# One class of 21 places for weights and working tiles, and the down stage's products into h issued later

## The chip, the cores and the metric

The kernel runs on one core of a Trainium2 chip. A core has five engines that run side by side, each through its own queue in order: TensorE (PE; its weight loads are shown as PEld), VectorE (DVE), ScalarE (ACT), GpSimd (POOL) and SyncE (SP). Here SyncE only issues transfers from memory to the on-chip buffer; 16 DMA engines move them. The metric is the device time of one execution in microseconds, lower is better. Three runs of the kernel before took 2260.67, 2268.3 and 2269.16 us, median 2268.3.

## The reference

256 tokens of width 1024 in float32 pass through two layers and then a third block:

```
for l in 0, 1:
    h = h + hybrid_mixer(rmsnorm(h))       # dilated + windowed attention, branches w_a, w_b, output w_o
    h = h + expert_choice_ffn(rmsnorm(h))  # 16 experts, each takes its 32 best tokens
h = rmsnorm(h)
token mixer: gated linear recurrence + long convolution (projections w2z, w2q, w2v, w2h, w2g ..., output w2o)
MoE: 32 experts in 4 groups, 2 experts per token; final norm

def expert_choice_ffn(h, w_router, w_gate, w_up, w_down):
    aff = softmax(h @ w_router); gate, idx = top_k(aff.T, 32)
    a, u = xe @ w_gate, xe @ w_up          # per expert, 1024 -> 1024 each
    ye = (silu(a) * u) @ w_down            # per expert, 1024 -> 1024
    return zeros.at[idx].add(gate * ye)
```

All expert weights are read in full: 128 MB of gate and up and 64 MB of down weights in each of the two layers, and about as much again in the MoE.

## The kernel before

**Stages.** Layer 0's mixer, layer 0's experts, layer 1's mixer, layer 1's experts, token mixer, MoE. An expert stage has two parts. In the first, for every expert, eight chunks of `w_eg` (gate and up together, 128 x 2048 floats, 1 MB, 8 KB per partition) are multiplied by the tokens the expert chose (L774). In the second, the down stage, for four column quarters q and four groups y of four experts, four chunks of `w_ed` are multiplied by the hidden values (L816), the result is scaled and split into two parts (`yd`, ScalarE L109 and VectorE L110), multiplied by the scatter matrix `Ge` (L824, the products into h), and added to h (VectorE, L827).

**Woven work.** Layer 0's down stage contains layer 1's first projections: `ahead.steps` is a generator of projection steps (weights `wk`, split by ScalarE, VectorE or GpSimd at L98 and L99, products at L118 to L120). From q = 1 on, 8, 8 and 7 steps are issued behind the products into h of groups 0, 1 and 2.

**Places.** A chunk is loaded into a place of the on-chip buffer, and the load waits until that place's last reader is done. Before, there are classes "w" (5 places) and "x" (4) and ten single places of the same 8 KB that also hold working tiles (`hTa`, `qa`, `V`, `G`, `hgw`, `hn`, `ob` ...). `chunk()` takes its class from a list written by hand (`K.spare` first, then the cycle `K.ring`). Some chunks are loaded in quarters (`quarters`, L68, 256 KB each) into places of the small classes P, PT, wh and wl. P holds attention probabilities, wh and wl hold the split weights of the projections, so a quarter there waits for the splits and products of the mixer before.

**What sets the order.** The program is written as one sequence; a list scheduler with a simulated time line places instructions on each engine's queue. SyncE then issues its loads in that order, at most eight behind each other on eight completion semaphores: a load also waits for the one eight places ahead of it to land, and a load that waits holds all behind it. Lines: `chunk` L48, `piece` with its load L60, `quarters` L68, experts L755 to L833, MoE chunks L1377 and L1422.

Of the kernel before, what the change touches and what calls it, by code (L numbers as in the profile page):

```python
# [9 lines left out]
F = mybir.dt.float32  # L10
FR = mybir.dt.float32r
# [8 lines left out]
L = 2  # L20
# [12 lines left out]
class Core:  # L33
    def __init__(self, ctx, tc, A):
# [6 lines left out]
        self.ring, self.spare, self.idle = list("wwxwx"), [], ()  # L41
# [16 lines left out]
    def piece(self, src, tag):  # L58
        t = self.sb.tile([128, PW], F, name="w", tag=tag, bufs=RING.get(tag, 1))
        self.nc.sync.dma_start(out=t[:, :src.shape[1]], in_=src)  # L60
        return t

# [12 lines left out]
    def t(self, shape, name, bufs=1, tag=None, dt=F):  # L75
        return self.sb.tile(shape, dt, name=name, tag=tag or name, bufs=bufs)
# [134 lines left out]
class Ahead:  # L211
# [6 lines left out]
    def start(self):  # L218
# [5 lines left out]
        self.raw = K.t([128, 8, T], "raw", RING["x"], tag="x")  # L224
# [65 lines left out]
RING = {"w": 5, "x": 4}  # L290
# [25 lines left out]
def mixer(K, h, l, ada, first=None, ahead=None):  # L316
# [142 lines left out]
    if ahead:  # L459
        K.ring = list("wwwwwx")  # L460

    def window():
        for pair in range(8):
            po = pos[pair % 2]
            PTs = []
            for half in range(2):
# [6 lines left out]
                sk = K.sink[:, l, hd, :]  # L473
# [45 lines left out]

    QS = [K.t([128, 8, T], "q0", tag="qc", dt=FR), K.t([128, 8, T], "q1", RING["x"], tag="x", dt=FR)]  # L520
    kx = K.t([128, 8, T], "kx", RING["x"], tag="x", dt=FR)
# [82 lines left out]
def spread_gate(K, g):  # L604
    nc = K.nc
    if g == 0:
        K.gt = K.t([128, PW], "gt", tag="x", bufs=RING["x"]).rearrange("p (a b) -> p a b", a=2)
# [10 lines left out]
def first_loads(K):  # L618
# [3 lines left out]
    K.sink, K.bgate = K.load("sink", [128, L, 16, 2]), K.load("bgate", [128, L, 16])  # L622
# [3 lines left out]
    K.iota, K.fold = K.load("iota", [128, 65]), K.load("fold", [128, 96])  # L626
# [54 lines left out]
def experts(K, h, l, mix, ada, prep, ahead=None):  # L681
# [74 lines left out]
    K.ring = list("wwxwx")  # L756
    K.spare = [None] * 7 + ["V", "qa", "qb", "qc"] + ([] if ahead else ["ob"]) + ["hgw"] + (["G"] if ahead else [])
    K.spare += [("P",) * 4] + ([] if ahead else ["hn"]) + [("wh", "wh", "wh", "wl"), ("wl", "wl", "PT", "PT")]
    hid, Ge = [], []
    gw = K.t([128, 4], "gw4")  # L760
    for e in range(NE):
        if e == 2:
            for _ in gather(1):
                pass
            K.ring = ["w", "x", "w", "V", "w", "x", "qb", "w", "qc", "x", "w", "hgw", "x", "G"] if ahead else list("wwxwx") + ["qc"]
        oh, xT = ohs[e // 8], xTs[e // 8]
        gu = K.bank("mm")
        for k in range(KD):
# [3 lines left out]
            w = K.chunk(A["w_eg"][l, e, k])  # L772
# [34 lines left out]
    K.ring = ["w", "x", "w", "qc", "w", "x", "w", "x", "w"] if ahead else ["w", "x", "w", "qc", "w", "hTa", "x", "w", "qa", "w"]  # L807
    for q in range(4):
        for y in range(NE // 4):
            ws = [K.chunk(A["w_ed"][l, q, 4 * y + x]) for x in range(4)]  # L810
            dn = K.bank("acc")
            for fb in range(8):
                for x in range(4):
# [7 lines left out]
            p = K.bank("sc")  # L821
            for tt in range(2):
                for i in range(2):
                    nc.tensor.matmul(p[:, tt * T:(tt + 1) * T], lhsT=Ge[y // 2][:, y % 2, tt * 128:(tt + 1) * 128],  # L824
                                     rhs=yd[:, i], start=(i == 0), stop=(i == 1))
            hs = h[:, :, q * T:(q + 1) * T]
            nc.vector.tensor_add(hs, p.rearrange("p (t c) -> p t c", t=2), hs)  # L827
# [5 lines left out]
    K.ring = list("wwxwx")  # L833
# [22 lines left out]
def context(K):  # L856
# [24 lines left out]
    s0 = K.t([128, PW], "S0", tag="x", bufs=RING["x"])  # L881
# [814 lines left out]
```

## Time and profile before

| | |
|---|---|
| median of three runs | 2268.3 us |
| profiled execution | 2264.96 us |
| its span (first to last instruction) | 2263.2 us |
| mean granted TensorE clock | 0.906 of 2.4 GHz |
| TensorE busy | 1810.0 us (80%) |
| VectorE, ScalarE, GpSimd busy | 786.9, 588.7, 220.7 us |
| moved from memory | 745.77 MB, mean 330 GB/s |
| median from issue to landing, w_eg and w2eg chunks | 15.6 and 19.8 us |

The stages lie in the span thus: layer 0's mixer to about 277 us, its expert products from 290 to 625, its woven down stage from 625 to 816; layer 1's mixer to 977, its experts to about 1480; the token mixer to about 1780; the MoE to the end at 2263.2. Because the limits differ from stage to stage, the shares of the whole span say little; the rows below are taken stage by stage. GB/s tells how far the transfers are the limit in a stretch, busy time how far an engine is, and the timelines tell when SyncE issued what.

### The profile page before, as it was taken

What the parts mean: (1) busy time and instruction counts of PE and PEld (TensorE: products, weight loads), DVE (VectorE), ACT (ScalarE), POOL (GpSimd) and SP (SyncE); (2) the same over time, 40 slices, a digit from 0 to 9 for tenths busy, and PEclk for the clock granted to TensorE, in tenths of its full rate; (3) what the DMA queues carried; (4) which work ended last, traced back from release to release, by engine and by line L of the source; (5) the groups of instructions that cost most, each with busy time, mean ns of one, the idle gap of its engine ahead of it and who ended that gap; (6) DMA issues with size and microseconds to landing.
All of it is one profiled execution on the core that took longest, in us unless ns stands there. A gap on an engine that the chain in (4) does not pass through costs nothing.

```text
span 2263.2 us, 30298 instructions
## 1 busy us (share of the span) xinstructions
PE 1810.0 (80%) x12172; PEld 1026.7 (45%) x12172; DVE 786.9 (35%) x1823; ACT 588.7 (26%) x1182; POOL 220.7 (10%) x179
## 2 busy tenths in 40 slices
PE   8999997666699998996778566669999877776765
PEld 8877741111277765842234223248888522121211
DVE  5766620000145589631211111147647511111112
ACT  5545510000033345620124200036325310000000
POOL 2111200000011122200000000024224100000000
PEclk9999997777799999998899777889999999999999
DMA  7446599999999944679999999982336799999996
GB/s 301 136 165 238 216 377 421 421 421 422 422 375 409 386 163 187 233 278 366 411 416 415 371 420 421 420 336 105 119 115 233 300 411 421 421 421 421 422 421 277
DMA packets 113626, 748.87 MB, mean 331 GB/s; under 512 B 14695, under 2 KB 15112, under 8 KB 25416
## 3 DMA queue, kind: packets, MB, share of 16 engines
q1 hardware_dynamic: 112936, 745.82, 81.7%
q8 instruction: 98, 1.61, 0.3%
q10 hardware_dynamic: 544, 1.05, 0.1%
q14 instruction: 48, 0.39, 0.1%
HBM read 745.77 MB, written 1.05 MB: 330 GB/s over the span
## 4 chain that ended last, share of the span: by engine, by line
PE 44%; DMA 27%; issue 21%; DVE 5%; ACT 2%; POOL 0%; POOLq 0%; SPq 0%; DVEq 0%; ACTq 0%
DMA w<-in_w_eg 15%; DMA w<-in_w_ed 7%; PE mm L118 7%; PE mm L120 7%; PE mm L119 6%; PE mm L774 4%; PE acc L816 4%; DMA w<-in_w2z 1%; DVE wl L99 1%; PE acc L493 1%; PE acc L901 1%; PE sc L841 1%; DMA w<-in_ada 1%; PE acc L1181 1%; PE sc L478 1%
## 5 line engine op out<-in xcount | busy, mean ns | idle before, releaser
L774 PE MATMUL mm<-w,xT 128*32 128x512 f32 x2048 | 325.0, 743 | 131.4 <-DMA w<-in_w_eg 131.3
L98 ACT ACTIVATE wh<-w 128x512 fp32r<-128x512 f32 x384 | 239.5, 630 | 314.5 <-PE mm L119 237.1
L118 PE MATMUL mm<-hTa,wh 128*128 128x256 f32 x960 | 282.5, 296 | 8.3 <-DVE qa L242 2.4
L120 PE MATMUL mm<-hTa,wl 128*128 128x256 f32 x960 | 276.4, 291 | 4.5 <-DVE wl L99 4.2
L119 PE MATMUL mm<-hTb,wh 128*128 128x256 f32 x960 | 274.4, 287 | 1.2 <-DVE hTb L1004 1.2
L99 DVE TENSOR_TENSOR wl<-w,wh 128x512 fp32r<-128x512 f32 x286 | 220.1, 775 | 100.4 <-ACT wh L98 97.5
L1429 PE MATMUL mm<-w,xT 128*32 128x512 f32 x1024 | 174.1, 618 | 61.5 <-DMA w<-in_w2eg 60.9
L99 POOL TENSOR_TENSOR wl<-w,wh 128x512 fp32r<-128x512 f32 x98 | 129.7, 1324 | 917.2 <-ACT wh L98 411.8
L774 PEld LDWEIGHTS mm<-w,xT 128*32 128x32 f32 x2048 | 59.1, 123 | 352.3 <-DMA w<-in_w_eg 245.3
L816 PE MATMUL acc<-w,hid 128*32 128x256 f32 x2048 | 167.0, 436 | 59.9 <-DMA w<-in_w_ed 59.9
L118 PEld LDWEIGHTS mm<-hTa,wh 128*128 128x128 f32 x960 | 182.8, 191 | 28.4 <-issue 13.5
L120 PEld LDWEIGHTS mm<-hTa,wl 128*128 128x128 f32 x960 | 182.5, 191 | 14.3 <-issue 6.2
L119 PEld LDWEIGHTS mm<-hTb,wh 128*128 128x128 f32 x960 | 183.5, 191 | 5.4 <-issue 2.4
L816 PEld LDWEIGHTS acc<-w,hid 128*32 128x32 f32 x2048 | 76.8, 124 | 136.2 <-DMA w<-in_w_ed 68.2
L1470 PE MATMUL acc<-w,work 128*32 128x512 f32 x512 | 103.4, 681 | 36.4 <-DMA w<-in_w2ed 35.0
L1429 PEld LDWEIGHTS mm<-w,xT 128*32 128x32 f32 x1024 | 33.6, 110 | 172.1 <-DMA w<-in_w2eg 126.1
L175 POOL TENSOR_TENSOR rs<-rs,mhalf 128x2 f32<-128x2 f32 x9 | 6.7, 748 | 1010.7 <-DVE rs L174 1010.5
L790 DVE TENSOR_TENSOR hid<-tp,sg 128x256 f32<-128x256 f32 x32 | 13.6, 424 | 221.0 <-ACT sg L789 221.0
L88 DVE COPY gs<-mm 128x512 f32<-128x512 f32 x16 | 11.1, 692 | 199.6 <-PE mm L774 199.6
L110 DVE SCALAR_TENSOR_TENSOR yd<-acc,gw,yd 128x256 fp32r<-128x256 f32 x32 | 15.5, 483 | 179.4 <-ACT yd L109 179.4
L789 ACT ACTIVATE sg<-tp 128x256 f32<-128x256 f32 x32 | 12.3, 383 | 227.5 <-PE tp L786 227.4
L109 ACT ACTIVATE yd<-acc,gw 128x256 fp32r<-128x256 f32 x32 | 15.1, 473 | 213.2 <-PE acc L816 213.2
(469 smaller groups left out, 2504.4 us busy)
## 6 DMA issues: line engine op xcount, KB each, us to landing
w<-in_w_eg SPq DMA_DIRECT2D x250, 1024.0 KB, 15.6
w<-in_w_ed SPq DMA_DIRECT2D x128, 1024.0 KB, 14.1
w<-in_w2eg SPq DMA_DIRECT2D x126, 1024.0 KB, 19.8
w<-in_w2ed SPq DMA_DIRECT2D x63, 1024.0 KB, 19.8
w<-in_ada SPq DMA_DIRECT2D x24, 1024.0 KB, 6.3
w<-in_w_in SPq DMA_DIRECT2D x22, 1024.0 KB, 7.1
w<-in_wk SPq DMA_DIRECT2D x20, 1024.0 KB, 9.3
w<-in_w_b SPq DMA_DIRECT2D x8, 1024.0 KB, 6.2
```

Of the source, the lines that this page charges most:

```text
L98: self.hi = nc.scalar.activation(hi, src, AF.Copy)
L99: (nc.gpsimd if n in self.idle or n % 4 == 3 else nc.vector).tensor_tensor(lo, src, hi.bitcast(F), OP.subtract)
L118: mm(out, lhsT=l[0], rhs=r[0], start=start, stop=False)
L119: mm(out, lhsT=l[0], rhs=r[1], start=False, stop=False)
L120: mm(out, lhsT=l[1], rhs=r[0], start=False, stop=stop)
L478: nc.tensor.matmul(p[:, sl], lhsT=q[hq], rhs=KL[hq, kv // 2, :], start=False, stop=True)
L493: nc.tensor.matmul(po[half * 64:half * 64 + 64, :T], lhsT=V[:, kt, c:c + 64], rhs=PTs[half][:, kt * 256:(kt + 1) * 256], start=(kt == 0), ...
L774: nc.tensor.matmul(gu[32 * j:32 * j + 32, :], lhsT=xT[:, k, (e % 8) * CAP:(e % 8 + 1) * CAP], rhs=w[:, j * 512:(j + 1) * 512], start=(k == ...
L816: nc.tensor.matmul(dn[32 * x:32 * x + 32, :T], lhsT=hid[e // 8][:, e % 8, f, hh * 32:hh * 32 + 32], rhs=ws[x][:, fb * T:(fb + 1) * T], sta ...
L841: nc.tensor.matmul(p[:, :T], lhsT=hn[:, tt, kb * 128:(kb + 1) * 128], rhs=oh[:, tt].rearrange("p a b -> p (a b)"), start=(tt == 0), stop=( ...
L1429: nc.tensor.matmul(gu[o:o + 32, :], lhsT=xT[:, k, y:y + CAP2], rhs=ws[x][:, (2 * kk + j) * 512:(2 * kk + j + 1) * 512], start=(k == 0), st ...
L1470: nc.tensor.matmul(dn[32 * x:32 * x + 32, :], lhsT=hid[x][:, c, :], rhs=wd[x][:, c * 512:(c + 1) * 512], start=(c == 0), stop=(c == 3), ti ...
```

## The change

The classes "w" and "x" and the ten single places become one class "W" with 21 places. A tile whose old name is in `WHOLE`, and every whole chunk, takes the next place of that class in turn; the lists `K.ring` are gone. `K.spare` is now the same at every expert stage and the MoE: eight whole chunks, two in quarters ("P","P","wh","wh") and ("wh","wl","wl","wl"), and then whole ones. The first 21 chunks of an expert stage (19 whole, two in quarters), and the first 19 of the MoE (17 whole), are requested in one go ahead of the stage's products. In the down stage the products into h and the add are a function `add`: in layer 0 from q = 1 on it is called behind 6, 6, 6 and 5 woven steps, elsewhere behind the next group's expert products. Room comes from smaller scratch tiles. The core of the diff:

```diff
 def chunk(self, src):
-        tag = self.spare.pop(0) if self.spare else None
-        if tag is None:
-            tag = self.ring[self.nchunk % len(self.ring)]
-            self.nchunk += 1
-        if isinstance(tag, tuple):
-            return self.quarters(src, tag)
-        return self.piece(src, tag)
...
+        if self.spare and (tags := self.spare.pop(0)):
+            return self.quarters(src, tags)
+        t = self.sb.tile([128, PW], F, name="w", tag="W", bufs=PLACES)
         self.nc.sync.dma_start(out=t[:, :src.shape[1]], in_=src)
         return t
...
-RING = {"w": 5, "x": 4}
+WHOLE = {"x", "hTa", "hTb", "qa", "qb", "qc", "V", "G", "hgw", "hn", "ob"}
+PLACES = 21
+SPARE = [None] * 8 + [("P", "P", "wh", "wh"), ("wh", "wl", "wl", "wl")]
...
-    K.ring = list("wwxwx")
-    K.spare = [None] * 7 + ["V", "qa", "qb", "qc"] + ([] if ahead else ["ob"]) + ["hgw"] + (["G"] if ahead else [])
-    K.spare += [("P",) * 4] + ([] if ahead else ["hn"]) + [("wh", "wh", "wh", "wl"), ("wl", "wl", "PT", "PT")]
+    K.spare = SPARE[:]
+
+    ws = [K.chunk(A["w_eg"][l, i // KD, i % KD]) for i in range(PLACES)]
...
-            w = K.chunk(A["w_eg"][l, e, k])
+            w = ws.pop(0) if ws else K.chunk(A["w_eg"][l, e, k])
...
+    def add(q, y, yd):
+        p = K.bank("sc")
+        for tt in range(2):
+            for i in range(2):
+                nc.tensor.matmul(p[:, tt * T:(tt + 1) * T], lhsT=Ge[y // 2][:, y % 2, tt * 128:(tt + 1) * 128],
+                                 rhs=yd[:, i], start=(i == 0), stop=(i == 1))
+        hs = h[:, :, q * T:(q + 1) * T]
+        nc.vector.tensor_add(hs, p.rearrange("p (t c) -> p t c", t=2), hs)
...
+            if late:
+                add(*late)
             yd = K.t([128, 2, T], "yd", NP, tag="PT", dt=FR)
             K.split_to(yd[:, 0], yd[:, 1], dn[:, :T], gw[:, y:y + 1])
...
-            if ahead and q and y < 3:
-                for _ in islice(ahead.steps, (8, 8, 7)[y]):
+            late = (q, y, yd)
+            if ahead and q:
+                for _ in islice(ahead.steps, (6, 6, 6, 5)[y]):
                     pass
+                add(*late)
+                late = None
...
+    K.spare = SPARE[:]
+    K.pre = [K.chunk(A["w2eg"][0 + 2 * i + x, c]) for i in range(2) for c in range(4) for x in range(2)]
+    K.pre += [K.chunk(A["w2ed"][x, 0]) for x in range(3)]
```

SyncE's queue at the end of layer 0's mixer, before (L60 is a whole chunk, L68 a quarter; `xN` is N such rows):

```order
56 L60 DMA w<-in_w_eg 128x2048 x2
57 L60 DMA w<-in_ada 128x2048
58 L60 DMA w<-in_w_eg 128x2048 x7
59 L68 DMA w_3379<-in_w_eg 128x512
60 L68 DMA w_3385<-in_w_eg 128x512
61 L68 DMA w_3391<-in_w_eg 128x512
62 L68 DMA w_3381<-in_w_eg 128x512
63 L68 DMA w_3393<-in_w_eg 128x512
64 L68 DMA w_3383<-in_w_eg 128x512
65 L60 DMA w<-in_w_eg 128x2048 x15
```

And after (L53 whole, L64 quarter):

```order
46 L64 DMA w_3246<-in_w_eg 128x512
47 L64 DMA w_3248<-in_w_eg 128x512
48 L53 DMA w<-in_w_o 128x2048 x2
49 L53 DMA w<-in_ada 128x2048 x3
50 L64 DMA w_3256<-in_w_eg 128x512
51 L64 DMA w_3250<-in_w_eg 128x512
52 L64 DMA w_3258<-in_w_eg 128x512
53 L64 DMA w_3252<-in_w_eg 128x512
54 L64 DMA w_3260<-in_w_eg 128x512
55 L64 DMA w_3254<-in_w_eg 128x512
56 L53 DMA w<-in_w_eg 128x2048 x126
```

All eight quarters of w_eg now stand ahead of its first whole chunk; two of them, in places of class P, also ahead of the last two w_o chunks. At the end of layer 1's mixer the rows are the same.

SyncE's queue at the end of the token mixer, before; seven whole w2eg chunks stand above these rows in ones and twos between the loads of the token mixer's own weights:

```order
209 L60 DMA w<-in_w2eg 128x2048 x3
210 L60 DMA w<-in_ada 128x2048 x3
211 L68 DMA w_13743<-in_w2eg 128x512
212 L68 DMA w_13737<-in_w2eg 128x512
213 L60 DMA w<-in_w2eg 128x2048
214 L68 DMA w_13745<-in_w2eg 128x512
215 L68 DMA w_13739<-in_w2eg 128x512
216 L68 DMA w_13747<-in_w2eg 128x512
217 L599 DMA gb<-in_gtb 128x512
218 L68 DMA w_13741<-in_w2eg 128x512
219 L68 DMA w_13749<-in_w2eg 128x512
220 L68 DMA w_13751<-in_w2eg 128x512
```

And after, where no w2eg stands above these rows:

```order
155 L53 DMA w<-in_ada 128x2048 x4
156 L64 DMA w_13596<-in_w2eg 128x512
157 L64 DMA w_13590<-in_w2eg 128x512
158 L64 DMA w_13598<-in_w2eg 128x512
159 L64 DMA w_13592<-in_w2eg 128x512
160 L64 DMA w_13600<-in_w2eg 128x512
161 L599 DMA gb<-in_gtb 128x512
162 L64 DMA w_13586<-in_w2eg 128x512
163 L64 DMA w_13594<-in_w2eg 128x512
164 L64 DMA w_13588<-in_w2eg 128x512
165 L53 DMA w<-in_w2eg 128x2048 x14
166 L53 DMA w<-in_w2ed 128x2048 x3
```

TensorE's queue in layer 0's down stage, the first group of q = 1, before (L816 the experts' down products, L824 the products into h, L118 to L120 the woven projections, `sc` and `acc` banks of the accumulator):

```order
1749 L119 MATMUL mm<-hTb,wh 128x256
1750 L120 MATMUL mm<-hTa,wl 128x256
1751 L816 MATMUL acc<-w,hid 32x256 x35
1752 L824 MATMUL sc<-yd,Ge_3821 128x256 x4
1753 L118 MATMUL mm<-hTa,wh 128x256
1754 L119 MATMUL mm<-hTb,wh 128x256
```

And after, the third group of q = 1 (L824 is now the down products, L810 the products into h, L117 to L119 the projections):

```order
1683 L119 MATMUL mm<-hTa,wl 128x256
1684 L824 MATMUL acc<-w,hid 32x256 x32
1685 L117 MATMUL mm<-hTa,wh 128x256
1686 L118 MATMUL mm<-hTb,wh 128x256
...
1706 L118 MATMUL mm<-hTb,wh 128x256
1707 L119 MATMUL mm<-hTa,wl 128x256
1708 L810 MATMUL sc<-yd,Ge_4308 128x256 x4
1709 L117 MATMUL mm<-hTa,wh 128x256
```

The products into h moved from directly behind their group's down products to behind some twenty rows of projections.

## Rows read from the trace of the kernel before

**Rows 1.** The page: bytes moved in 40 slices (GB/s), and one row of the DMA issues.

```profile
GB/s 301 136 165 238 216 377 421 421 421 422 422 375 409 386 163 187 233 278 366 411 416 415 371 420 421 420 336 105 119 115 233 300 411 421 421 421 421 422 421 277
...
w<-in_w_eg SPq DMA_DIRECT2D x250, 1024.0 KB, 15.6
```

**Rows 2.** Stage windows: length, busy us of each engine, PEclk, DMA share, GB/s.

```profile
270.00:300.00 30.00, 25.68 (x142) 11.73 (x142) 15.20 (x51) 7.15 (x14) 0.71 (x1) 0.83 0.68 255
300.00:400.00 100.00, 80.03 (x487) 24.46 (x488) 9.40 (x24) 8.60 (x17) 0.00 (x0) 0.80 1.01 418
500.00:625.00 125.00, 76.80 (x548) 21.43 (x541) 9.68 (x17) 6.89 (x14) 0.00 (x0) 0.76 1.01 421
625.00:816.00 191.00, 180.55 (x1660) 141.41 (x1659) 103.76 (x166) 62.60 (x110) 28.07 (x22) 0.98 0.91 369
966.00:977.00 11.00, 10.53 (x48) 6.89 (x47) 3.50 (x6) 3.31 (x7) 1.29 (x1) 1.00 0.48 172
977.00:1040.00 63.00, 55.46 (x334) 24.45 (x332) 17.29 (x49) 11.50 (x23) 0.71 (x1) 0.92 0.81 313
1040.00:1240.00 200.00, 147.76 (x832) 58.95 (x832) 35.04 (x83) 49.66 (x75) 0.69 (x1) 0.87 1.01 415
1240.00:1440.00 200.00, 126.52 (x1076) 54.30 (x1072) 22.73 (x50) 24.64 (x38) 0.00 (x0) 0.79 0.98 407
1780.00:1820.00 40.00, 33.92 (x224) 14.52 (x222) 13.81 (x59) 10.50 (x19) 0.71 (x1) 0.91 0.82 313
2000.00:2200.00 200.00, 143.56 (x788) 42.16 (x782) 32.47 (x62) 14.61 (x27) 0.00 (x0) 0.97 1.01 421
```

**Rows 3.** SyncE's timeline, layer 0: start us, us, then the operation.

```profile
113.08 0.33 SPq L60 DMA_DIRECT2D w<-in_w_eg  x1
...
199.94 0.33 SPq L60 DMA_DIRECT2D w<-in_w_eg  x1
...
230.73 35.59 SPq L60 DMA_DIRECT2D w<-in_w_eg  x7
266.90 3.37 SPq L68 DMA_DIRECT2D w<-in_w_eg  x6
278.76 34.48 SPq L60 DMA_DIRECT2D w<-in_w_eg  x15
```

**Rows 4.** SyncE's timeline before the experts of layer 1.

```profile
851.49 0.33 SPq L60 DMA_DIRECT2D w<-in_w_eg  x1
...
948.16 17.55 SPq L60 DMA_DIRECT2D w<-in_w_eg  x4
972.57 0.33 SPq L68 DMA_DIRECT2D w<-in_w_eg  x1
```

**Rows 5.** SyncE's timeline before the MoE.

```profile
1601.27 0.33 SPq L60 DMA_DIRECT2D w<-in_w2eg  x1
...
1778.17 1.40 SPq L68 DMA_DIRECT2D w<-in_w2eg  x3
```

**Rows 6.** SyncE's timeline at the program's start.

```profile
5.74 3.02 SPq L60 DMA_DIRECT2D w<-in_w_in  x5
8.81 0.65 SPq L621 DMA_DIRECT2D negd<-in_negd  x1
```

**Rows 7.** ScalarE's timeline at the program's start.

```profile
17.63 1.15 ACT L98 ACTIVATE wh<-w 128x512 fp32r<-128x512 f32 x2 [2.68 <-issue]
```

**Rows 8.** Waits of TensorE's weight loads, 640 to 816: us, times, longest.

```profile
PEld sc L824 <- ACT yd L109: 4.4, 4, 1.1
PEld tp L190 <- DVE h L827: 2.7, 3, 1.0
...
PEld sc L824 <- DVE yd L110: 1.3, 4, 0.3
```

**Rows 9.** Waits of TensorE's products, 640 to 816: us, times, longest.

```profile
PE mm L118 <- DVE qa L242: 2.4, 2, 2.0
```

**Rows 10.** TensorE's timeline at the token mixer's start.

```profile
1501.07 1.94 PE L595 MATMUL acc<-w,cs 128*32 128x512 f32 x8 [9.29 <-DMA w<-in_ada]
```

More of the change, by code (lines that the diff above doesn't have):

```diff
@@ L40, in __init__ @@
         self.after = nullcontext
-        self.ring, self.spare, self.idle = list("wwxwx"), [], ()
+        self.idle, self.spare = (), []
     def load(self, name, shape, dt=F):
@@ L75, in t @@
     def t(self, shape, name, bufs=1, tag=None, dt=F):
-        return self.sb.tile(shape, dt, name=name, tag=tag or name, bufs=bufs)
+        tag = tag or name
+        if tag in WHOLE:
+            tag, bufs = "W", PLACES
+        return self.sb.tile(shape, dt, name=name, tag=tag, bufs=bufs)
     def copy(self, out, in_, scale=None, eng=None):
@@ L472, in window @@
                 m = K.t([128, 4], "m", 3)
-                sk = K.sink[:, l, hd, :]
+                sk = K.sink[:, l, hd:hd + 1].to_broadcast([128, 2])
                 for tt in range(2):
@@ L621, in first_loads @@
     nc.sync.dma_start(out=K.negd, in_=A["negd"])
-    K.sink, K.bgate = K.load("sink", [128, L, 16, 2]), K.load("bgate", [128, L, 16])
+    K.sink, K.bgate = K.load("sink", [128, L, 16]), K.load("bgate", [128, L, 16])
     K.gffn = K.load("gffn", [128, L, KD])
@@ L625, in first_loads @@
     nc.sync.dma_start(out=K.wr, in_=A["wr"])
-    K.iota, K.fold = K.load("iota", [128, 65]), K.load("fold", [128, 96])
+    K.iota, K.fold = K.load("iota", [128, CAP2 + 1]), K.load("fold", [128, 96])
     ada_setup(K)
@@ L818, in experts @@
                                      tile_position=(0, 32 * x))
+            if late:
+                add(*late)
             yd = K.t([128, 2, T], "yd", NP, tag="PT", dt=FR)
             K.split_to(yd[:, 0], yd[:, 1], dn[:, :T], gw[:, y:y + 1])
[L821 to L827, printed above, removed]
-            if ahead and q and y < 3:
-                for _ in islice(ahead.steps, (8, 8, 7)[y]):
-                    pass
+            late = (q, y, yd)
+            if ahead and q:
+                for _ in islice(ahead.steps, (6, 6, 6, 5)[y]):
+                    pass
+                add(*late)
+                late = None
             elif not ahead:
                 next(prep, None)
-    K.ring = list("wwxwx")
+    if late:
+        add(*late)
 def gather_x(K, xT, hn, oh, gain, bias=None):
@@ L1006, in token_mixer @@
     K.transposed(hn, emit_h)
-    cb = K.t([128, 4, 256], "cb", tag="cA")
+    cb = K.t([128, 5, 256], "cb", tag="cA")
+    K.small = cb[:, 4]
     K.tri, K.rmask, K.bmask = cb[:, 0], cb[:, 1:3], cb[:, 3].bitcast(I32).rearrange("p (d t) -> p d t", d=2)
@@ L1300, in moe @@
     cmb, msk, slot = R[:, 0], R[:, 1], R[:, 2]
-    lg = K.t([128, 2, 36], "lg2")
+    lg = K.small[:, 0:72].rearrange("p (t e) -> p t e", t=2)
     for tt in range(2):
@@ L1304, in moe @@
                                        op0=OP.mult, op1=OP.add)
-    s = K.t([128, 2, 64], "rsm")
+    s = K.small[:, 72:168].rearrange("p (t e) -> p t e", t=2)
     m, sm, pg, den = s[:, :, 0], s[:, :, 1], s[:, :, 2], s[:, :, 3]
@@ L1321, in moe @@
     le = lg[:, :, NG:36].rearrange("p t (g e) -> p t g e", g=NG)
-    tmp = K.t([128, 2, NE2], "rtmp")
+    tmp = K.small[:, 168:232].rearrange("p (t e) -> p t e", t=2)
     nc.vector.tensor_tensor(tmp.rearrange("p t (g e) -> p t g e", g=NG), le,
@@ L1325, in moe @@
     nc.vector.tensor_reduce(el, tmp.rearrange("p t (g e) -> p t e g", g=NG), axis=AX.X, op=OP.add)
-    ix = K.t([128, 2, 8], "ix")
+    ix = K.small[:, 232:248].rearrange("p (t e) -> p t e", t=2)
     ixu = K.t([128, 2, 8], "ixu", dt=mybir.dt.uint32)
@@ L1421, in moe_quad @@
         for c in range(4):
-            ws = [K.chunk(A["w2eg"][e + 2 * pr + x, c]) for x in range(2)]
+            ws = [K.next_chunk(A["w2eg"][e + 2 * pr + x, c]) for x in range(2)]
             for kk in range(2):
@@ L1463, in moe_quad @@
         end = e + 4 + hf == NE2 + 1
-        wd = [K.chunk(A["w2ed"][e + x, hf]) for x in range(3 if end else 4)]
+        wd = [K.next_chunk(A["w2ed"][e + x, hf]) for x in range(3 if end else 4)]
         if end:
@@ L1574, in constants @@
     o["ident"] = np.eye(128, dtype=f)
-    o["iota"] = np.broadcast_to(np.arange(65, dtype=f), (128, 65))
+    o["iota"] = np.broadcast_to(np.arange(CAP2 + 1, dtype=f), (128, CAP2 + 1))
     s = np.arange(128)
```

35 lines of the change are left out of this document (13 added, 22 removed).

## The prediction

> **What bounds the kernel now.** I read the page's slices first. Wherever the moved-bytes line stands at 420 or so, the transfers set the pace; wherever it drops, TensorE or a chain does [rows 1]. The stage table makes that sharp [rows 2]. In the expert products of layer 0 (500 to 625 us) and in the last MoE (2000 to 2200) the DMA engines move 421 GB/s all the time, while TensorE is busy for 77 of 125 us and 144 of 200. A weight chunk is 1024 KB [rows 1], so it costs 1.049 MB / 421 GB/s = 2.49 us, and every chunk of transfer that a neighbouring stage loses or gains moves the end of such a stage by 2.49 us. In the woven down stage (625 to 816) TensorE is busy for 181 of 191 us and the bytes fall to 369 GB/s: there a TensorE stall counts and a chunk does not.
>
> Next I read SyncE's own timeline, since it issues nearly every transfer in program order. Before the quartered chunks of layer 0 (six quarters from 266.90) it has already issued 12 whole w_eg chunks: one at 113.08, one at 199.94 ... and the last seven from 230.73 to 266.32 (groups in between hold the other three) [rows 3]. In layer 1 it is 11, from 851.49 to 965.7, ahead of the first quarter at 972.57 [rows 4]; before the MoE 11 as well, from 1601.27 on (seven groups of one to three), all ahead of the last three quarters, which end at 1779.57 [rows 5]. That is a head start taken from mixer time, in which the transfers have room.
>
> **The change part by part.**
>
> *One class of places.* The order of after puts the two quartered chunks of each expert stage on SyncE in front of every whole chunk of that stage. Their eight quarters go into the small classes P, wh and wl, which come free only with the last splits and products of the mixer's output projection. Before shows when that is: the quarters, which want the same classes, left at 266.90 to 270.27, from 972.57, and up to 1779.57 [rows 3 to 5]. The whole chunks behind them need no place of that kind (most wait only for the chunk eight places ahead to land), but they stand behind. So the head start goes; in exchange nothing stalls for places behind the transition, since 19 whole chunks (17 in the MoE) then follow at once.
>
> - Layer 0: of the 12 chunks the last is still in flight at 267, so 11 x 2.49 = 27.4 us of transfer move behind that time. Back come the idle transfer time of 270 to 300 (30 x (1 - 255/421) = 11.8 us) and of 300 to 400 (0.7) [rows 2], and two quarters in P that go early (two of four of one chunk, 1.2 us). Net +13.7 us. The rest of the stage runs at 421 in both. Bounds: 27.4 if none of the idle time comes back, 0 if the products did not need the chunks.
> - Layer 1: again 27.4 - 1.2. Back come the last 4 us of 966 to 977 (4 x (1 - 172/421) = 2.4), 977 to 1040 (63 x (1 - 313/421) = 16.2), 1040 to 1240 (2.9) and 1240 to 1440 (6.7), together 28.2 [rows 2]. Net -2; from -8 (a few chunks of the head start were not needed) to +10 (over a third of the idle time stays).
> - MoE: ten chunks landed and one among the quarters, 27.4 us in all. Back come 40 x (1 - 313/421) = 10.2 from 1780 to 1820 [rows 2]. Net +17.2. Nothing later gives it back: 2000 to 2200 is full at 421, with TensorE waiting. Bounds +10 and +27.
> - First loads: the 16 small ones now stand before the first whole w_in chunk, which was issued at 5.74 us; five chunks took SyncE 3.02 us and the first small load 0.65 [rows 6]; at 0.45 each, my estimate, sixteen take 7.2 us. One chunk in quarters still goes ahead. ScalarE split that first whole chunk at 17.63 [rows 7], 11.9 us behind its issue, so 4.7 us of this are left for the landing, two chunk times. I take +1, from 0 to +4.
> - Down stage to token mixer: two dfi loads and gb, which waits for the square of the final h, now stand before four ada and four w2z, which had begun earlier. Sincos and gf, on which the last norm waits, stand ahead of them instead of among them. Before, TensorE waited 9.29 us for one of the ada chunks there [rows 10], so it was late anyway. I take 0; from -2 to +12 (ada and w2z then come as one chain, five chunk times of 2.49 late).
>
> *Products into h issued later.* In the woven stage TensorE's queue now holds six steps of projection between a group's expert products and its products into h, so the wait for the split disappears: 4.4 us on ScalarE's yd and 1.3 on VectorE's [rows 8], 5.7 in all. The transposes that wait for h after the add lose about 2.3 of 2.7 [rows 8]. Together -8 us; at least 0 (the next stall is the projections' own, as on qa, 2.4 us [rows 9], and may grow into the gap), at most -10, since 181 of 191 us are busy [rows 2]. That h is finished a little later costs nothing while six steps follow. In layer 1 the same edit saves nothing: that stage waits for transfers.
>
> Smaller edits (sink unduplicated, scratch in one tile, iota halved) are some ten instructions on engines with room: 0. The TensorE clock in the woven stage is 0.98 of 2.4 GHz, so no more than 2% of 181 us is to be had.
>
> Sum: +13.7 - 2 + 17.2 + 1 + 0 - 8 = +22. On the profiled execution's 2264.96 us this is 2287; the median of the runs shown, 2268.3, lies 3.3 above it and inside their own scatter of 2260.67 to 2269.16.
>
> The rate is where the Trainium skill differs ("DMA: Bandwidth & Descriptors", Specifications): it gives about 358 GB/s per core for HBM. By that a chunk would cost 2.93 us and the eleven 32 us instead of 27. The rows show 421 for hundreds of microseconds, so the measurement decides.
>
> **The rivals.**
>
> *A: the queue is not held, and the places repay.* If whole chunks reached the engines before the quarters' places come free, the head starts stay and the idle time closes: -12.5 - 28.2 - 10.2 - 8 + 1 = -58, that is 2207. For it speaks that 51 us of transfer time are really idle [rows 2]; against it that in before, too, SyncE's timeline has the later whole chunks only behind their quarters, at 278.76 [rows 3]. The point that decides: whole w_eg chunks on SyncE before 260 us, or w2eg before 1765. With the head starts kept before layer 1 and the MoE alone, 2287 - 2 x 27.4 = 2232.
> The skill speaks against A as well (same page, Anatomy of one DMA): a semaphore wait is spent on the issuing sequencer before dispatch, so what stands behind a waiting DMA is not queued yet.
>
> *B: no change.* The woven stage returns more: all that its 181 us busy leave of 191, 10 us, instead of 8, and layer 1 ends at its lower bound, -8, and the MoE at its lower bound, +10: 2264.96 + 13.7 - 8 + 10 + 1 - 10 = 2272. For it: the deeper pool lets w_ed and w_in run ahead in a stage that has (1 - 369/421) x 191 = 24 us of transfer to spare [rows 2]. Against it: nothing in the MoE's rows has slack to take 7 us.
>
> *C: slower still.* The wait in front of ada and w2z costs its upper bound, +12 on top: 2299. For it: the wait for ada already there [rows 10]; against: the same transfers land at about the same time by my reckoning. It decides if TensorE's first projection of the token mixer stands over 10 us further behind the last expert product than in before.
>
> **How the numbers follow.** Forecast (2276 to 2296) 0.52, A 0.11 (faster), B 0.24 (mostly within 0.5%), C 0.13. About 0.5%, 11 us, is what a measurement of this kernel can tell from no change, so the bounds stand at 2257 and 2279.6. Faster: A and a little of B, 0.13. Within: most of B and the low edge of the forecast, 0.23. Slower: 0.64. The range 2262 to 2302 leaves out A below and the far end of C, about 0.15 to 0.2.
>
> **What would show it.** SyncE's timeline should have no whole w_eg chunk before 266, none before 972 in layer 1's time (moved by a few us), no w2eg before 1779; the windows behind each transition should read 420 GB/s instead of 255 and 313. L810 on TensorE should wait for yd nearly nowhere between 640 and 830. The last expert product of layer 0 should come about 14 us later, the token mixer's start about 5 later, and the MoE's end some 22 later. I am wrong if whole chunks run before the quarters, if the woven stage shrinks by far more than 8 us, or if the end of the MoE is not paced by transfers at 421.

## The result and the profile after

The changed kernel takes 2344.8 us (median of 4 runs, 2341.3 to 2348.3) against 2268.7 for the kernel before: a ratio of 1.034, 95% interval 1.031 to 1.037. It is 76 us slower; I had forecast 2287, that is +22, with 2302 as the upper end. The direction was right, the size was not.

To see where the 76 us lie I lined up the two profiled executions by TensorE products: both have 12172, and the N-th product of one stands at nearly the same point of the program as the N-th of the other. The lag is how much later it starts in the changed kernel, in us. This table is worked out from the traces; its last columns are three of the experiments below (p2: the second part alone; e1: the one class without quartered chunks; e4: three waits fewer than e1). Each column is one execution: e4 to e7, which have the same order of TensorE's products up to product 1900, lag at 1950 by 5.3 to 12.3, so no single entry is good to better than some us.

```
product  before at  what ends there             after    p2     e1     e4
  150      28.9 us  first w_in chunk used        +4.2   +0.3   +4.3   +4.4
 1950     309.7     mixer of layer 0            +15.8   +0.1  +15.3   +5.3
 2250     361.6     start of its experts        +33.2   +1.2  +14.5   +5.0
 3100     596.0     its expert products         +34.3   +1.7  +16.8   +6.0
 5000     829.2     woven down stage            +23.4   -4.9   +4.1   -5.1
 5700     947.7     mixer of layer 1            +37.1   -8.4  +21.3  +10.7
 6250    1064.6     start of its experts        +39.1   -9.3   +6.0   -5.9
 8250    1466.0     experts, most of down       +39.1  -12.0   +6.2   -6.3
 8800    1559.7     first z of token mixer      +54.8  -11.1  +15.9   -0.5
10250    1773.0     token mixer                 +63.0  -12.6  +24.0   +7.4
10700    1864.1     start of the MoE            +81.7  -11.9  +23.4   +2.9
12150    2244.6     MoE                         +83.3  -11.0  +27.2   +6.9
```

The profiled execution of the changed kernel is its longest one (2348.3 us, span 2346.5), so its last row is +83 where the medians differ by 76. By the table the loss is: head and mixer of layer 0 +16, start of its experts +17, woven stage -11, mixer of layer 1 +14, its experts +2, start of the token mixer +16, its rest +8, start of the MoE +19, the rest +3. The four entries for the mixers are 54 us, where my sum had 1.

The page of the changed kernel, beside [rows 1]: GB/s in 40 slices of 58.7 us.

```profile
GB/s 343 110 124 91 146 420 420 420 420 420 419 419 419 408 158 1 153 340 399 419 419 420 419 419 419 413 318 90 73 90 166 254 418 420 419 420 420 419 420 281
```

The sixteenth slice (880 to 939 us) has 1 GB/s: in layer 1's mixer the transfers stand still for 60 us, and the slices around it are thin. The changed kernel moves 420 GB/s in the stages behind each transition, as I had said, and little in those in front of it, which I had priced only by the expert chunks that move.

SyncE's own timeline, layer 0, beside [rows 3] (start, length of the group, line, what is loaded, count; L64 quarters, L53 whole chunks; `...` marks rows left out):

```profile
205.92 14.40 SPq L64 DMA_DIRECT2D w<-in_w_o  x8
220.42 1.33 SPq L53 DMA_DIRECT2D w<-in_w_b  x3
258.85 1.48 SPq L64 DMA_DIRECT2D w<-in_w_eg  x2
...
283.26 3.57 SPq L64 DMA_DIRECT2D w<-in_w_eg  x6
286.88 63.41 SPq L53 DMA_DIRECT2D w<-in_w_eg  x31
```

And layer 1, beside [rows 4]:

```profile
951.74 7.75 SPq L64 DMA_DIRECT2D w<-in_w_o  x7
959.54 1.92 SPq L53 DMA_DIRECT2D w<-in_w_b  x3
986.43 1.48 SPq L64 DMA_DIRECT2D w<-in_w_eg  x2
...
1010.65 3.59 SPq L64 DMA_DIRECT2D w<-in_w_eg  x6
1014.30 63.73 SPq L53 DMA_DIRECT2D w<-in_w_eg  x31
```

From the last norm of layer 1 into the MoE, beside [rows 5] and [rows 10]:

```profile
1510.52 20.79 SPq L1084 DMA_DIRECT2D dfi<-in_dfti  x2
1537.92 0.33 SPq L599 DMA_DIRECT2D gb<-in_gtb  x1
1538.30 1.85 SPq L53 DMA_DIRECT2D w<-in_ada  x4
1540.20 1.97 SPq L53 DMA_DIRECT2D w<-in_w2z  x4
...
1837.40 3.10 SPq L64 DMA_DIRECT2D w<-in_w2eg  x5
1840.56 0.42 SPq L599 DMA_DIRECT2D gb<-in_gtb  x1
...
1842.45 22.46 SPq L53 DMA_DIRECT2D w<-in_w2eg  x14
```

In each there is no whole expert chunk before the quarters, as forecast, and what stands behind a group of quarters leaves within 0.1 us of the last one (283.26 + 3.57 = 286.83, and the first whole w_eg at 286.88): it was ready and stood in the queue. The Trainium skill says so too ("DMA: Bandwidth & Descriptors", Anatomy of one DMA, a section on the GpSimd path: a semaphore wait is spent on the sequencer that issues, before dispatch), and these groups, which SyncE issues, agree with it. What I had not followed is that not only expert chunks stand there. Three w_b chunks, which the end of the mixer needs, stand behind eight quarters of w_o in both layers, and all ada and w2z chunks behind dfi and gb. Whether that costs time is another question; e3, e7 and e11 below ask it.

Windows of the changed kernel, beside [rows 2] (length, then busy time with instructions for TensorE, its weight loads, VectorE, ScalarE and GpSimd, then granted clock, DMA share, GB/s):

```profile
287.00:317.00 30.00, 24.84 (x139) 13.16 (x140) 15.27 (x55) 6.67 (x14) 0.71 (x1) 0.83 1.01 402
890.00:950.00 60.00, 58.83 (x305) 35.56 (x302) 48.58 (x176) 29.75 (x100) 14.08 (x10) 0.91 0.00 1
1014.00:1040.00 26.00, 20.34 (x115) 8.93 (x116) 13.41 (x41) 6.87 (x14) 0.71 (x1) 0.87 1.00 390
```

The stretches behind the quarters are now full (402 and 390 where before had 255 and 313), and still the start of layer 0's experts costs 17 us beyond the mixer's lag, where I had 14. The idle time came back nearly as counted; why the loss is 3 us more no run here tells.

### The profile page after: what moved, and what is told of

It reads as the page before. It is cut to its first block, busy times and chain, and to the rows that moved or that the text cites. A ratio compares the mean times of both kernels' runs of the same rounds, so it can differ in the third digit from the quotient of the medians.

```text
span 2346.5 us, 30288 instructions
## 1 busy us (share of the span) xinstructions
PE 1863.1 (79%) x12172; PEld 1041.7 (44%) x12172; DVE 782.0 (33%) x1823; ACT 584.4 (25%) x1181; POOL 217.9 (9%) x179
## 5 line engine op out<-in xcount | busy, mean ns | idle before, releaser
L773 PE MATMUL mm<-w,xT 128*32 128x512 f32 x2048 | 339.9, 760 | 129.5 <-DMA w<-in_w_eg 129.0
L97 ACT ACTIVATE wh<-w 128x512 fp32r<-128x512 f32 x384 | 234.7, 628 | 301.4 <-PE mm L118 211.3
L117 PE MATMUL mm<-hTa,wh 128*128 128x256 f32 x960 | 286.5, 300 | 13.6 <-ACT wh L97 9.5
L119 PE MATMUL mm<-hTa,wl 128*128 128x256 f32 x960 | 278.6, 295 | 7.5 <-DVE wl L98 6.6
L118 PE MATMUL mm<-hTb,wh 128*128 128x256 f32 x960 | 277.5, 290 | 1.6 <-DVE hTb L109 1.6
L98 DVE TENSOR_TENSOR wl<-w,wh 128x512 fp32r<-128x512 f32 x286 | 212.3, 756 | 112.3 <-ACT wh L97 109.5
L1436 PE MATMUL mm<-w,xT 128*32 128x512 f32 x1024 | 177.6, 617 | 72.0 <-DMA w<-in_w2eg 71.4
L824 PE MATMUL acc<-w,hid 128*32 128x256 f32 x2048 | 179.9, 449 | 63.9 <-DMA w<-in_w_ed 63.9
L773 PEld LDWEIGHTS mm<-w,xT 128*32 128x32 f32 x2048 | 50.1, 121 | 354.1 <-DMA w<-in_w_eg 306.3
L117 PEld LDWEIGHTS mm<-hTa,wh 128*128 128x128 f32 x960 | 187.8, 196 | 35.0 <-ACT wh L97 15.6
L119 PEld LDWEIGHTS mm<-hTa,wl 128*128 128x128 f32 x960 | 185.1, 195 | 20.6 <-DVE wl L98 9.1
L118 PEld LDWEIGHTS mm<-hTb,wh 128*128 128x128 f32 x960 | 188.0, 196 | 5.2 <-issue 2.8
L824 PEld LDWEIGHTS acc<-w,hid 128*32 128x32 f32 x2048 | 79.9, 128 | 147.9 <-DMA w<-in_w_ed 84.2
L1436 PEld LDWEIGHTS mm<-w,xT 128*32 128x32 f32 x1024 | 34.5, 110 | 194.8 <-DMA w<-in_w2eg 143.5
L1477 PEld LDWEIGHTS acc<-w,work 128*32 128x32 f32 x512 | 20.9, 121 | 106.8 <-issue 59.1
```

The costliest lines, as they stand in the source:

```text
L97: self.hi = nc.scalar.activation(hi, src, AF.Copy)
L98: (nc.gpsimd if n in self.idle or n % 4 == 3 else nc.vector).tensor_tensor(lo, src, hi.bitcast(F), OP.subtract)
L117: mm(out, lhsT=l[0], rhs=r[0], start=start, stop=False)
L118: mm(out, lhsT=l[0], rhs=r[1], start=False, stop=False)
L119: mm(out, lhsT=l[1], rhs=r[0], start=False, stop=stop)
L773: nc.tensor.matmul(gu[32 * j:32 * j + 32, :], lhsT=xT[:, k, (e % 8) * CAP:(e % 8 + 1) * CAP], rhs=w[:, j * 512:(j + 1) * 512], start=(k == ...
```

## The experiments

All times are medians beside runs of the kernel before in the same series (2262.7 to 2265.7 us); each ratio has its 95% interval. Lags are worked out as in the table above.

**p2: only the second part, on the kernel before** (the products into h issued later; the diff's `add`, `late` and the new step counts, places as before).

> The kernel before, with the second part of the change alone: products into h behind 6, 6, 6, 5 woven steps in layer 0 and behind the next group's products elsewhere; places as before. Queue theory (the loss of 76 us comes from SyncE standing at loads whose places come free late, the second part is a small gain): 8 to 11 us faster than before, about 2258, all of it between 640 and 816 us. Rival (the late products into h hold up what follows): slower than before by 10 us or more, with TensorE waiting at layer 1's mixer or at the token mixer's start.

2249.3 us, ratio 0.994 (0.992 to 0.996). The lag is within 2 us of 0 until the woven stage, -4.9 behind it, -12.0 at the end of layer 1's down stage and -11.0 at the end. The waits of TensorE's weight loads on yd [rows 8] are gone; of its products this is now the longest wait between 640 and 816 us (total, times, longest):

```profile
PE mm L119 <- DVE hTb L110: 1.6, 1, 1.6
```

So the second part is a gain by itself, 13 us by the medians, and this version beats both kernels.

**p1: only the first part** (the changed kernel with the old order of the down stage).

> The changed kernel with the first part alone: one class of 21 places, products into h issued where they were before. Queue theory: 8 to 11 us slower than the changed kernel, about 2354. Rival (the late products cost): faster than the changed kernel, below 2335.

2354.9 us, ratio 1.040 (1.037 to 1.044; two runs). With the second part, the changed kernel is 10 us faster by the medians, which come from two series, and 14 by the ratios: the two parts about add, and the one class alone costs some 90.

**p3: the small edits alone, on the kernel before** (sink unduplicated, iota halved, the router's scratch in one tile, smaller DMA scratch).

> The kernel before with the small edits alone: sink without its double and broadcast, router scratch in one tile, shorter iota, smaller scratch for dynamic transfers. My cost of them was 0: within 5 us of before, 2258 to 2268, mixers unchanged. Rival (they, not the places, lengthen the mixers): 10 to 30 us slower, in the mixers.

2265.6 us, ratio 1.0002 (0.999 to 1.0015). They cost nothing that these runs can tell, some 3 us at most.

**e1: the changed kernel without quartered expert chunks.**

```diff
-SPARE = [None] * 8 + [("P", "P", "wh", "wh"), ("wh", "wl", "wl", "wl")]
+SPARE = []
-    ws = [K.chunk(A["w_eg"][l, i // KD, i % KD]) for i in range(PLACES)]
+    ws = [K.chunk(A["w_eg"][l, i // KD, i % KD]) for i in range(PLACES - 2)]
-    K.pre += [K.chunk(A["w2ed"][x, 0]) for x in range(3)]
+    K.pre += [K.chunk(A["w2ed"][x, 0]) for x in range(1)]
```

(and the down stage's last chunk of the MoE whole).

> The changed kernel without the quartered chunks of the expert stages and the MoE (the last w2ed chunk whole too), 19 and 17 whole chunks requested ahead instead. Queue theory: the first whole w_eg chunk leaves SyncE behind w_o and ada instead of behind the last splits, some ten chunks are there again when the experts start; layer 0's expert stage loses at most 8 us to before instead of 19, layer 1's stage gains 5 to 15; in the MoE the load gb, whose place waits for the last residual add, still stands in front, so 15 to 24 us stay lost there. Total 2300 to 2325. Rival (one class handed out in turn makes chunks wait for the longest-lived tile wherever they stand in the queue): within 6 us of the changed kernel, 2339 to 2351, and SyncE's whole chunks no earlier.

2294.7 us, ratio 1.014 (1.011 to 1.017; two runs): of the 76 us some 44 (each against the kernel before in its own series) to 50 (by the two medians) are gone with the quarters. SyncE's first whole expert chunks in layer 0, layer 1 and the MoE now are

```profile
225.42 123.28 SPq L53 DMA_DIRECT2D w<-in_w_eg  x40
...
950.35 99.51 SPq L53 DMA_DIRECT2D w<-in_w_eg  x34
...
1784.65 0.33 SPq L599 DMA_DIRECT2D gb<-in_gtb  x1
1785.03 26.30 SPq L53 DMA_DIRECT2D w<-in_w2eg  x16
```

61, 64 and 57 us earlier than in the changed kernel, and the three starts of the experts cost -1, -15 and -1 us by the table instead of +17, +2 and +19. In layer 1 the mixer still grows a lag of 17 us (+4 to +21; 14 in the changed kernel), but the start of the experts gives 15 of it back: whole w_eg chunks go out from 950 us, ahead of product 5700 at 969, and that stage waits for transfers, so a late mixer costs only what it keeps from the queue. With the quarters, which wait for the mixer's end, its lag stays.

**e2: e1, and gb in the class PT instead of P** (`gb = K.t([128, 512], "gb", NP, tag="PT")`): in e1 gb is the load that all w2eg stand behind.

> As the one without quarters, and gb in a place of class PT, which comes free earlier than one of class P. Queue theory: w2eg chunks leave SyncE some 10 to 25 us before the last residual add, and ada and w2z before the square of the final h; the MoE gains 10 to 20 us and the token mixer's start 3 to 8 against the kernel without quarters alone: 2280 to 2308. Rival (places in turn): no gain over it, within 5 us.

2284.3 us, ratio 1.009 (1.006 to 1.012). w2eg goes out from 1751.0 instead of 1785.0 and at product 10700 e2 is 9 us ahead of e1 (+14.1 against +23.4), 6 of them gained since product 10250, in the MoE's start. One 256 KB load of gb in the wrong class cost e1 some 10 us.

**e3: e2, and the chunks of w_o whole** (`ws = [K.chunk(A["w_o"][l, 2 * c + i]) for i in range(2)]`), so that w_b no longer stands behind their quarters.

> As the kernel without quarters and with gb in PT, and the first two w_o chunks of each mixer whole instead of in quarters. Queue theory: w_b and w_o leave SyncE without the wait for the window attention's last P and PT places, so TensorE has no wait of 2.6 us on the split of w_b before the branch products; each mixer shortens by 3 to 6 us and w_eg leaves a little earlier; 2272 to 2280 against 2284. Rival (the mixers are slower because of what the attention's own order does, not because of these loads): 2281 to 2288.

2289.5 us (2281.8 to 2291.6), ratio 1.010 (1.006 to 1.014): not faster than e2 by the runs. In the profile the last three w_b chunks are out by 196 us (e2: from 218), and layer 0's mixer still has its lag (+15.8). So w_b's queue was not what made that mixer late: a miss.

**e4: e3, and the five ada steps of each mixer behind its window attention.**

```diff
-    weave((gates(), 8), (islice(ada, 5), 5), (window(), 20))
+    weave((gates(), 8), (window(), 20))
+    for _ in islice(ada, 5):
+        pass
```

> As the kernel with whole w_o, and the five ada steps of each mixer issued behind the gate projections and the window attention instead of woven into them. Theory (ada chunks that are loaded early and used late hold places that the last w_in and wk chunks want, so that TensorE runs the window attention with no projection to fill between): from 140 to 150 us some 30 or more projection products instead of 2, layer 0's mixer 5 to 8 us shorter and layer 1's 5 to 15: 2255 to 2270. Rival (the last projections are late for another reason): within 5 us of the kernel with whole w_o, or slower by the ada products that no longer hide.

2273.0 us (2271.2 to 2286.0), ratio 1.005 (1.001 to 1.008). SyncE in layer 0, e3 first:

```profile
44.24 0.33 SPq L53 DMA_DIRECT2D w<-in_ada  x1
...
119.32 10.79 SPq L53 DMA_DIRECT2D w<-in_w_in  x2
...
152.64 0.33 SPq L53 DMA_DIRECT2D w<-in_w_in  x1
```

and e4:

```profile
55.91 51.64 SPq L53 DMA_DIRECT2D w<-in_w_in  x7
116.53 43.83 SPq L53 DMA_DIRECT2D w<-in_ada  x5
```

In e3, as in the changed kernel, four ada chunks are fetched from 44 us on and used from 137 us on, and the last three w_in chunks, which the projections need, go out at 119 to 153 us instead of by 108. With ada behind, layer 0's mixer lags by 5.3 us, 4.4 of them the head's. (The three kernels below have the same order of TensorE there, and the lag is 12.3, 8.2 and 8.9; in e1 to e3 and the changed kernel it is 13.8 to 15.8: the gain is some 2 to 10 us.) Layer 1's mixer stays as late.

So moving the ada steps is a gain: 2 to 10 us in layer 0 by the traces, 16 over the whole by the medians of e3 and e4, whose intervals overlap. My reason for it, that early ada chunks hold places that w_in needs, is not shown by it, since the edit moves ada's products in TensorE's order as well. And the kernel before speaks against it: its layer 0 has no such lag, though its last three w_in chunks leave at 123, 137 and 158 us (the first of them as the second of a pair), no earlier than e3's at 119, 130 and 153. What makes layer 0's mixer late is thus not known.

```profile
116.89 6.29 SPq L60 DMA_DIRECT2D w<-in_w_in  x2
...
137.01 0.33 SPq L60 DMA_DIRECT2D w<-in_w_in  x1
...
158.00 0.33 SPq L60 DMA_DIRECT2D w<-in_w_in  x1
```

**e5, e6, e7: three waits more, each taken away from e4 alone.** e5 puts the loads of the scans' masks (L1018 to L1020 of the changed kernel, which wait for layer 1's last window softmax) behind the last norm's; e6 puts layer 1's last projections ahead of its window attention; e7 puts dfi behind the first w2ga chunk.

In e5 (`got` is the load of gf; rmask and bmask likewise):

```diff
-    nc.sync.dma_start(out=K.tri, in_=A["tri"])
+    with tc.issue_after(got.ins):
+        nc.sync.dma_start(out=K.tri, in_=A["tri"])
```

In e6, for layer 1 (and the window scores are put behind the last projection issued so far):

```diff
-    weave((project_w(), 5), (dilated(), 8))
-    weave((gates(), 8), (window(), 20))
+    weave((chain(project_w(), gates()), 13), (dilated(), 8))
+    weave((window(), 20))
```

In e7 (`K.sent` is the last whole chunk's load):

```diff
-            nc.sync.dma_start(out=dfi[i], in_=A["dfti"][:, i])
+            with K.tc.issue_after(K.sent.ins):
+                nc.sync.dma_start(out=dfi[i], in_=A["dfti"][:, i])
```

> The kernel of e4 (2273.0 us, span 2270.6), with one change: the three loads of the scans' masks (tri, rmask, bmask), which wait for the last window softmax of layer 1 and stood ahead of three w_b chunks, four w_o chunks and every whole w_eg chunk, are put behind the last norm's loads at the end of layer 1. Theory 1 (the queue is held by the masks): w_b goes out before 890 us instead of 923, w_eg some 15 us before 936, and layer 1's mixer ends 8 to 12 us earlier: 2261 to 2266. Theory 2 (the w_b chunks wait for places of their own, which the last projections and the ada products give back at about the same time): w_b moves by at most 20 us but nothing waits for it, layer 1's mixer keeps its lag within 4 us: 2269 to 2275. I expect theory 2.

> The kernel of e4, with one change: in layer 1's mixer the last projections (84 products) are put ahead of the window attention in TensorE's order, where the kernel before has most of them, instead of inside and behind it. Theory 1 (the order is the cause of layer 1's lag: the window attention runs thin at a low clock, and the projections come after it): the lag that grows over layer 1's mixer, +19 us in e4, falls under +8, the mean granted clock from 820 to 880 us rises over 0.8, and the total is 2257 to 2264. Theory 2 (the lag comes from what stands behind in the queue, w_b and w_o, so an earlier end of the projections only lengthens the wait for them): lag still +15 to +19, 2270 to 2275. I expect theory 1.

> The kernel of e4, with one change: the two dfi loads, which wait for the last products into h and stood ahead of four ada and four w2z chunks at the start of the token mixer, are put behind the first w2ga chunk. Theory 1 (they hold the queue): the ada chunks go out at about 1464 instead of 1483 us, w2z likewise, and the lag of 5 us that e4 gains between the last expert products and the first projections of the token mixer goes: 2267 to 2270. Theory 2 (TensorE waits there for the norm of h, and the chunks land in time anyway): the queue moves but the first projection stays at 1510 us, 2271 to 2275. I expect theory 1, with little certainty.

2275.9, 2274.9 and 2279.2 us (ratios 1.004, 1.003 and 1.007; intervals 1.002 to 1.005, 1.002 to 1.005 and 1.004 to 1.009): none is faster than e4, which itself had missed my 2255 to 2270 by 3 us. In e5 all four w_b chunks are out by 906 us (in e4 three of them leave from 923), w_eg goes from 929.64 instead of 936.06, and layer 1's mixer grows the lag as before (+14.5 from product 5000 to 5700; e4 +15.8): theory 2. In e6 the mixer is quicker in the middle; here are 820 to 880 us of before, e4 and e6:

```profile
820.00:880.00 60.00, 52.80 (x366) 39.36 (x364) 57.03 (x156) 33.09 (x71) 17.56 (x12) 0.97 0.49 177
```

```profile
820.00:880.00 60.00, 51.95 (x267) 38.11 (x264) 47.97 (x179) 32.23 (x88) 2.52 (x2) 0.72 0.17 59
```

```profile
820.00:880.00 60.00, 47.44 (x307) 40.34 (x305) 47.08 (x142) 28.75 (x62) 15.55 (x12) 0.80 0.20 71
```

Before has 366 products in that time at a clock of 0.97, e4 267 at 0.72, e6 307 at 0.80, and its lag at product 5250 is +5.0 instead of +11.3. But at the mixer's end it is +11.7 (e4 +10.7): the gain is gone, so my theory 1 fell there. In e7 ada goes out at 1467.75 instead of 1483.42 and nothing follows from it, since TensorE waits there for the norm of h (11.25 us in e4, 11.24 in e7; in before its wait there was for ada, 9.29 [rows 10]); theory 1 fell here too.

**e9: e4 with all three, and five whole w_in chunks ahead of the small loads.**

> e4 with the three edits of e5, e6 and e7, and the first five whole w_in chunks issued ahead of the small loads at the head, as in the kernel before. If the mixers' lag is made of these four (the head 4 us, layer 1's order 10 to 16, the token mixer's start 2 to 5, the masks 0 to 4) the time is 2247 to 2257, faster than the kernel before by some 10 us and about equal to p2 (2249), that is: the one class of places costs nothing when no load that waits stands ahead of what is needed, and gains nothing. If the places themselves cost in the mixers, it stays above 2262. The head's part alone shows as a lag at the first 150 products of under 1 us instead of 4.3.

2270.1 us, ratio 1.002 (1.001 to 1.003). The head's lag is +2.2 (+0.6 and -0.6 in e10 and e11, which have the same head) instead of +4.4, layer 1 ends at -8.1, and then the token mixer loses 15 us (-8.1 to +6.5) where p2, with the old places, loses none. It missed 2247 to 2257: the waits that I had found are not all that the one class costs.

**e10, e11, a1: the two longest stands of SyncE in the token mixer.** In e9 the router's weights leave 50 us behind the chunk before them (1674.71 and 1724.39 us), in the changed kernel too. e10 is e9 with `K.wr = K.t([128, KD, 64], "wr2", tag="x")`, a place of the one class; e11 is e10 with gb there as well; a1 is the changed kernel with the edit of e10.

> The kernel of e9 (2270.1 us, span 2268.8), with one change: the router's weights of the MoE are loaded into a place of the one class instead of the tile that the gate vector of the token mixer still uses; in e9 that load leaves at 1724.39 us, 50 us behind the chunk before it, and one w2b chunk, four w2o, four ada and all w2eg chunks stand behind it, while the transfers are idle from 1675 to 1724. Theory 1 (that load is what holds the queue in the token mixer): w2b and w2o go out before 1700 us, w2eg before 1720 instead of 1738, the 5 us that are lost between products 10150 and 10250 go, and the MoE starts with more chunks landed: 2256 to 2264. Theory 2 (the chunks behind it wait for their own places at nearly the same time): 2267 to 2272. I expect theory 1.

> e10, and gb of both gates in a place of the one class as well: in e9 gb leaves at 1499.18 us, 21 us behind the w2z chunk before it, with three w2z, two w2q and two w2v chunks behind it. If that wait costs the 3 to 5 us that the first projections of the token mixer lose against the kernel before (products 8500 to 8800), this is 3 to 5 us under e10, and e10 and this one together reach 2251 to 2260. If the first projections wait for the norm of h anyway, it equals e10 within 2 us.

> The changed kernel itself (2344.8 us, span 2346.5), with the one edit of e10: the router's weights in a place of the one class. In the changed kernel that load stands from 1730.95 to 1780.61 us with w2b, w2o and ada behind it, and the lag against the kernel before grows by 5 us there (57.6 to 63.0 at products 10000 to 10250). Theory 1: that growth goes, 2336 to 2341, and the 20 us at the MoE's start stay, since the quarters wait for the last products of the output projection. Theory 2: the quarters' wait decides all, 2343 to 2348.

2269.5, 2270.5 and 2346.7 us (ratios 1.002, 1.002 and 1.036; intervals 1.001 to 1.003, 1.001 to 1.003 and 1.034 to 1.038). The stand is gone, SyncE in e10:

```profile
1673.43 13.65 SPq L53 DMA_DIRECT2D w<-in_w2b  x2
1695.92 0.33 SPq L1279 DMA_DIRECT2D wr<-in_wr  x1
...
1734.78 56.94 SPq L53 DMA_DIRECT2D w<-in_w2eg  x16
```

and the lag from product 8250 to 10250 is +14.2 as in e9, in a1 +23.8 as in the changed kernel (+23.9). A load that stands for 50 us cost nothing that these runs can tell: w2eg goes out only 4 us earlier without that stand (1734.78 against 1738.39), and TensorE did not gain from the earlier w2b and w2o. With gb moved as well (e11) the first projections are no earlier either.

So the 14 to 15 us that the one class costs inside the token mixer stay open. From product 9500 to 10250 e10 takes 126 us, p2 116; these are the windows, e10 first:

```profile
1652.00:1779.00 127.00, 119.27 (x756) 102.43 (x756) 70.34 (x128) 55.63 (x115) 44.22 (x35) 0.96 0.52 194
```

```profile
1644.00:1761.00 117.00, 113.27 (x759) 99.19 (x759) 74.23 (x128) 56.79 (x116) 47.31 (x36) 1.00 0.59 219
```

Nearly the same number of products, 10 us more: 6 of them in busy time, at a lower clock (0.96 against 1.00), and 4 in small gaps; no long wait. In the first projections (e10 1506 to 1585 us, p2 1505 to 1577) TensorE waits more often for the splits of the w2 chunks, e10 first:

```profile
PE mm L119 <- DVE wl L98: 3.9, 5, 2.4
```

```profile
PE mm L120 <- DVE wl L99: 1.6, 1, 1.6
```

Over all the projections (e10 1507 to 1722 us, p2 1507 to 1710) the waits of TensorE's products come to 12.2 us against 6.5. The scheduler has put each engine's instructions in another order there; which of these orders costs the time no run here tells. The 14 us of layer 1's mixer are open in the same way; without the quarters the experts behind it give them back.

## Why the prediction was wrong

- **The failed step is the sum's silence on the mixers.** "Down stage to token mixer: I take 0", "First loads +1", and no term at all for the inside of the three mixers. Measured: +16 up to the end of layer 0's mixer, +14 in layer 1's, +16 at the start of the token mixer and +8 in it, 54 us in all, where the sum had 1. I had followed only the expert chunks through the queue. But a class that chunks share with working tiles changes where many loads stand, and the order of all engines with it. What of that costs time the runs show in part. The small loads now ahead of the first whole w_in chunk cost 2 to 5 us (with five w_in chunks ahead of them again the head's lag falls from +4.2 to +2.2, +0.6 and -0.6 in e9 to e11). The ada steps woven into layer 0's mixer cost 2 to 10 us (e4), by places or by order. The rest of layer 0's mixer, layer 1's mixer and 14 to 15 us in the token mixer stay open.
- **The rule behind the +13.7 and +17.2 was right, and shown.** No whole expert chunk goes ahead of the quarters, and without the quarters both losses vanish (e1). Measured are +17 and +19, so that the forecast slower was not luck. When the quarters are gone, gb in P holds w2eg in their place (e2), which I had not seen.
- **First loads, +1, came out as +4.2,** at the edge of my 0 to +4: the first whole w_in chunk left at 15.42 us instead of 5.74, 9.7 later where I had estimated 7.2.
- **Layer 1's experts, -2, came out as +2** against the lag of their mixer (+37.1 to +39.1), inside my -8 to +10: the idle time did come back (390 to 420 GB/s). What I had not seen is that the quarters tie the stage to its mixer's end, so that the mixer's +14 stays. In e1 a mixer as late is given back.
- **The second part, -8:** right in kind; of the 5.7 us of weight loads waiting on yd 1.3 are left in the changed kernel. It is -11 in the changed kernel's woven stage and -13 in all alone (p2, by the medians). "In layer 1 the same edit saves nothing" may be wrong by some 3 us (-8.4 to -12.0 in p2, one execution).
- **The small edits, 0:** shown (p3), within 3 us.
- **Rivals.** A (the queue is not held) is what e1 makes of the kernel in part, and even there the mixers keep it above before. C named the right place (+16 where it had +12 as its upper bound); its reason is not borne out: in e7, which has no quarters, the wait for dfi is gone and the place still loses 8 us (-1.5 to +6.6), and in e11, with gb's wait gone too, 10 (-8.2 to +1.8). In the changed kernel itself this was not tried. B did not happen.
- The range ended at 2302 because I bounded each term that I had and gave none to what I had not. My three signs of being wrong had the same gap: the quarters did go first, the woven stage shrank by 11 us and the MoE's end runs at 420 GB/s, so none of them showed, and the time was still 54 us over.

## What to carry to other kernels

When a change alters which loads share a class of places, follow every load on the issuing queue through every stage, and the order of the engines too, not only the loads that the change is about: a load that waits for its place holds whatever stands behind it, but that costs time only where something behind it is needed next. A stage that transfers pace forgives a late stage in front, unless its first transfers wait for that stage's end; so never let a small class that comes free last hold the first loads of the next stage. And take the two parts of a change apart before keeping either: here one was worth 13 us and the other cost some 90.

## What the runs showed that I had not expected

A wait of TensorE can cost more than its own length. In e4, layer 1's mixer, TensorE waits 2.46 us for a softmax at 830 us, after a wait of 1.02 us, and the score products behind it are slower one by one (start, length of the group, count; the wait in brackets):

```profile
824.77 0.70 PE L438 MATMUL sc<-qa 64*128 64x256 f32 x2
...
832.36 1.94 PE L448 MATMUL tp<-ident,P 128*128 128x128 f32 x8 [2.46 <-DVE P L422]
834.23 1.22 PE L438 MATMUL sc<-qa 64*128 64x256 f32 x2
```

The two windows around it:

```profile
824.00:830.00 6.00, 4.86 (x40) 3.64 (x38) 5.81 (x23) 5.39 (x13) 0.00 (x0) 1.00 0.09 36
830.00:845.00 15.00, 12.64 (x54) 10.27 (x54) 11.57 (x36) 4.46 (x10) 1.26 (x1) 0.54 0.21 70
```

From 830 to 845 us the granted clock is 0.54, nearly all of it the 1.2 GHz level, and the same two products take 1.22 us instead of 0.70. In before, with 366 products from 820 to 880 us where e4 has 267, the clock is 0.97. I had priced a wait at its own length only, and a change of order at nothing.
